# Gate and up of four SwiGLU layers: the high and low parts of the tokens beside each other, 512 moving columns at once

## The chip, the cores and the metric

The kernel runs on one core of one Trainium2 chip. The metric is the device time of one execution in microseconds (us), as the median of several runs. Smaller is better.

## The reference, cut to what matters

Two residual blocks run over 256 tokens of width 1024 in float32: in order a SwiGLU layer (here f1), an attention mixer (m1), a SwiGLU (f2), a second mixer (ab), a SwiGLU (f3), a third mixer (cd), a SwiGLU (f4) and a last norm. The change touches the four SwiGLU layers, each with a hidden width of 2816:

```python
D_MODEL = 1024
SEQ = 256
D_FF = 2816
def _swiglu(x, w_gate, w_up, w_down):
    return (jax.nn.silu(x @ w_gate) * (x @ w_up)) @ w_down
...
        f = _swiglu(_rmsnorm(x, ffn1_pre_g[l]), ffn1_w_gate[l], ffn1_w_up[l], ffn1_w_down[l])
        x = x + 0.5 * _rmsnorm(f, ffn1_post_g[l])
```

## The kernel before, in words

Every operand of a matmul is split in two float32r parts, a high one (`xh`, `wh`, `hh`) and a low one (`xl`, `wl`, `hl`), and each product is made of three matmuls: high by high, high by low, low by high (`mm3`, L506).

**Weights.** `Stream` loads weight tiles of 128x1024 (512 KB) in the order of a list (`ffn_specs`, L140) through SP's DMA queue. ACT casts each to `wh` (L91) and DVE, a few times POOL, subtracts to get `wl` (L96). There are 4 raw buffers and 6 of each part; `take(n)` (L111) hands out n tiles and emits the casts and subtractions that come into buffers which the tiles before have left.

**Tokens.** `enter` (L447) normalises, transposes through the PE (`to_t`, L353, tile `tp`) and writes `xh` (ACT, L364) and `xl` (DVE, L369), 128 partitions by 8 chunks of the width by 256 tokens, in two tiles (`new_xt`, L346).

**A SwiGLU layer** (`ffn`, L588) walks over 11 blocks of 256 hidden columns. Block 0 is computed inside `enter` by `first(h, mid)` (L604), once for each half h of the tokens: tokens stationary, weights moving with 256 columns, 48 matmuls into the bank `fh`, where `mid` puts the second half's transposes among the first half's matmuls. For blocks 1 to 10, `gemm_b` (L516) computes gate and then up with weights stationary and tokens moving: for each of two groups of 128 hidden columns 8 chunks by 3 products, so 48 matmuls of 256 columns, in one bank `gb`. Then ACT takes silu (L651), DVE multiplies by up (L652), ACT and DVE split the result into `hh` and `hl` (L622, L623), and `down` (L570) multiplies the block before with the down weights: 24 matmuls of 512 columns in the banks `f`. The last `down` takes the blocks 9 and 10 together.

In three of the four layers POOL copies `xh` and `xl` three times (L637, tile `xc`) to places chosen by byte offsets (`COPIES_AT`), and `act_x` picks one of the copies for each block. `XT_AT`, `COPY_PAD` and `HH_AT` are further offsets of tiles in a partition. `hooks` adds work of the later mixers behind some blocks of f1 and f3.

The order of each engine's work is that of the code. `ws.take` stands at the head of every `gemm_b` and `down`, so its casts and subtractions stand ahead of what the code emits later.

Of the kernel before, what the change touches and what calls it, by code (L numbers as in the profile page):

```python
# [8 lines left out]
F32 = mybir.dt.float32  # L9
# [5 lines left out]
P = 128  # L15
# [11 lines left out]


XT_AT = ((192, 240), (0, 256), (0, 256), (0, 0), (192, 240), (0, 256), (192, 192), (192, 240), (0, 256), (32, 32))
COPY_PAD = {0: 0, 1: 0, 3: 0}  # L30
HH_AT = (32, 32, 288, 32)

COPIES_AT = {0: ((192, 192), (64, 64), (320, 320)), 1: ((128, 128), (256, 256), (448, 192)),
             3: ((384, 384), (192, 320), (320, 64))}
# [105 lines left out]
def ffn_specs(wg, wu, wd):  # L140
    out = []
    d = w_d(wd)
    for j in range(11):
        out += w_b(wg, 256 * j) + w_b(wu, 256 * j)
        if 0 < j < 10:
            out += d[2 * j - 2:2 * j]
    return out + d[18:22]
# [43 lines left out]
class Kern:  # L191
    def __init__(self, ctx, tc, A, out, phases):
        self.ctx, self.tc, self.nc, self.A, self.out = ctx, tc, tc.nc, A, out
        self.phases = phases
        nc = self.nc
        pool = lambda n, b, **k: ctx.enter_context(tc.tile_pool(name=n, bufs=b, **k))
        self.const = pool("const", 1)
        self.w_raw = pool("wraw", NB_RAW)
        self.w_h = pool("wh", NB_HL)
        self.w_l = pool("wl", NB_HL)  # L200
        self.xt_p = pool("xt", 1)
        self.g_p = pool("gain", 2)
        self.tmp = pool("tmp", 2)
        self.sm = pool("sm", 4)
        self.mm_p = pool("mm", 8, space=bass.MemoryType.PSUM)
        self.specs = self.all_specs()
        self.ws = Stream(nc, (self.w_raw, self.w_h, self.w_l), self.specs)
        self.gains = {}
        self.bg = []
        self.fin = None  # L210
        self.after = 3

# [10 lines left out]
    def all_specs(self):  # L223
        A = self.A
        sp = []
        for ph in self.phases:
            if ph in ("f1", "f2"):
                k = ph[1]
                sp += ffn_specs(A[f"ffn{k}_w_gate"], A[f"ffn{k}_w_up"], A[f"ffn{k}_w_down"])
            elif ph in ("f3", "f4"):  # L230
                k = int(ph[1]) - 3
                sp += ffn_specs(A["ffn_w_gate_2"][k], A["ffn_w_up_2"][k], A["ffn_w_down_2"][k])
# [113 lines left out]
    def new_xt(self):  # L346

        self.nxt = getattr(self, "nxt", -1) + 1
        self.xh, self.xl = (
            self.xt_p.tile([P, 8 * S + 64], F32R, name=n, tag=n)[:, o // 4:o // 4 + 8 * S].rearrange("p (a t) -> p a t", a=8)  # L350
            for n, o in zip(("xh", "xl"), XT_AT[self.nxt]))

# [162 lines left out]

    def gemm_b(self, K=8, act=None):  # L516
# [71 lines left out]
    def ffn(self, gpre, gpost, coef, gnext, hooks=None, cut=False):  # L588
        nc = self.nc
        tt = nc.vector.tensor_tensor  # L590
        with self.tc.tile_pool(name="ffn", bufs=3) as fp:
            self.php = fp
            self.nff = getattr(self, "nff", -1) + 1
            fp.tile([P, HH_AT[self.nff] // 4], F32, name="gap", tag="gap", bufs=1)
            sets = {}
# [8 lines left out]
            def first(h, mid):  # L604
                if h == 0:
                    st["w"] = self.ws.take(4)
                p = self.ps(f"fh{h}")
                t = slice(h * P, (h + 1) * P)
                for i in range(2):
                    w = st["w"][2 * i:2 * i + 2]  # L610
                    prods = [((self.xh[:, k, t], self.xl[:, k, t]), (w[k // 4][0][:, k % 4, :], w[k // 4][1][:, k % 4, :]))
                             for k in range(8)]
                    self.mm3(p[:, i * S:(i + 1) * S], prods, True, True, True, mid if i else None)
                sg = fp.tile([P, S], F32, name="sgf", tag="sgf", bufs=2)
                nc.scalar.activation(out=sg, in_=p[:, 0:S], func=AF.Silu)
                tt(out=sg, in0=sg, in1=p[:, S:2 * S], op=ALU.mult)
                st[h] = sg

            def split(t, j):
                hh = fp.tile([P, 2, S], F32R, name="hh", tag="hh")  # L620
                hl = fp.tile([P, 2, S], F32R, name="hl", tag="hl")
# [3 lines left out]

            self.enter(gpre, first)
            self.gain(gnext)
            if gpost:
                self.gain(gpost)
            if self.nff in COPIES_AT:  # L630
                for n, at in enumerate(COPIES_AT[self.nff]):
                    sets[n] = []
                    for i, o in enumerate(at):
                        t = fp.tile([P, 8 * S + 128], F32R, name=f"xc{n}{i}", bufs=1)
                        o = (o + COPY_PAD[self.nff]) % 512 // 4
                        v = t[:, o:o + 8 * S].rearrange("p (a t) -> p a t", a=8)
                        nc.gpsimd.tensor_copy(out=v, in_=(self.xh, self.xl)[i])  # L637
                        sets[n].append(v)
            for j in range(1, 11):
                act_x = sets.get((j - 3) // 3)  # L640
                gt = self.gemm_b(act=act_x)
# [7 lines left out]
                up = self.gemm_b(act=act_x)  # L649
                sg = fp.tile([P, 2, S], F32, name="sg", tag="sg", bufs=2)  # L650
                nc.scalar.activation(out=sg, in_=gt, func=AF.Silu)  # L651
                tt(out=sg, in0=sg, in1=up, op=ALU.mult)  # L652
# [13 lines left out]
    def mixer1(self, gnext):  # L666
        nc, A = self.nc, self.A
        tt = nc.vector.tensor_tensor
        with ExitStack() as st:
# [4 lines left out]
            T([P, 8], "gap")  # L674
# [976 lines left out]
def _layout(inputs):  # L1651
# [4 lines left out]
    for n in ("ffn1_w_gate", "ffn1_w_up", "ffn1_w_down", "w_qkv", "w_out", "ffn2_w_gate", "ffn2_w_up", "ffn2_w_down", "x",  # L1656
              "ab_w_in_2", "ab_gate_a_w_2", "ab_gate_x_w_2", "ab_w_out_2", "cd_w_in_2", "cd_glu_w_2", "cd_w_out_2"):
        A[n] = A[n][0]
    rows = []
# [46 lines left out]
```

## Time and profile before

| | |
|---|---|
| runs | 1140.99 us median of 3 (1133.97 to 1141.59) |
| profiled execution, its own time | 1140.84 us |
| its span, first to last instruction | 1139.0 us |
| PE matmul busy | 1108.5 us (97%), 7435 instructions |
| PE weight load busy | 1008.6 us (89%) |
| DVE busy | 695.6 us (61%) |
| ACT busy | 547.5 us (48%) |
| POOL busy | 392.0 us (34%) |
| mean granted TensorE clock | 0.984 |

Busy time counts an instruction from its start to its end. Matmuls overlap in the pipeline, so the pace of the PE is read from the distance between starts, or from the chain of work that ended last, which counts each stretch once. A matmul named `gb<-xc,wh` writes the bank `gb` and reads `xc` and `wh`.

### The profile page before, as it was taken

The numbers are of one execution on the slowest core, as the hardware profiler recorded it, in microseconds if no ns is written. First come the engines' busy times: TensorE is split into PE (matmuls) and PEld (weight loads), VectorE is DVE, ScalarE is ACT, GpSimd is POOL, SyncE is SP. The second block draws the span as 40 slices with busy tenths as digits, with TensorE's granted clock in tenths as the row PEclk, the third lists the DMA queues.
The fourth block names the chain that finished last, engine by engine and source line by source line (L and its number), as shares of the span: only waits on it lengthen the run. The fifth ranks groups of instructions, "written<-read, shape, count | busy, mean of one in ns | idle before, by whom it ended". The sixth has DMA issues, their size and how long they took to land.

```text
span 1139.0 us, 18759 instructions
## 1 busy us (share of the span) xinstructions
PE 1108.5 (97%) x7435; PEld 1008.6 (89%) x7435; DVE 695.6 (61%) x828; ACT 547.5 (48%) x794; POOL 392.0 (34%) x590
## 2 busy tenths in 40 slices
PE   8999999989999999999989999999999999999997
PEld 7999999767889999997976999999989989999997
DVE  6765455789577554557573666556577557554554
ACT  4456445546555443445664544434353365443442
POOL 4206600655332000004151599999315126000000
PEclk9999999989999999999988999999999899999999
DMA  7865665642057556555621665575543335756551
GB/s 216 268 190 173 193 205 166 208 166 75 20 168 230 180 164 215 185 167 174 212 85 38 185 222 180 154 217 154 184 158 128 130 89 174 239 166 215 185 172 58
DMA packets 134361, 190.99 MB, mean 168 GB/s; under 512 B 6017, under 2 KB 109441, under 8 KB 134274
## 3 DMA queue, kind: packets, MB, share of 16 engines
q1 hardware_dynamic: 133536, 187.72, 52.5%
q0 software_dynamic: 736, 2.08, 0.7%
q8 instruction: 58, 0.95, 0.3%
q14 instruction: 29, 0.24, 0.1%
q10 hardware_dynamic: 2, 0.00, 0.0%
HBM read 188.73 MB, written 1.05 MB: 167 GB/s over the span
## 4 chain that ended last, share of the span: by engine, by line
PE 87%; DVE 5%; POOL 3%; issue 2%; ACT 1%; DMA 1%; SPq 0%; POOLq 0%; DVEq 0%; ACTq 0%
PE gb L514 45%; PE f L514 20%; PE wo L514 4%; PE fh L514 4%; PE ga L514 2%; PE gh L514 2%; PE o L842 1%; PE lg L514 1%; DVE x L397 1%; PE lt L1073 1%; DMA wraw<-in_ffn_w_up_dram 1%; PE y L1410 1%; PE pT L822 1%; PE M L1333 1%; PE sE L1379 1%
## 5 line engine op out<-in xcount | busy, mean ns | idle before, releaser
L96 DVE TENSOR_TENSOR wl<-wraw,wh 128x1024 fp32r<-128x1024 f32 x323 | 412.8, 1302 | 171.4 <-ACT wh L91 167.0
L91 ACT CAST wh<-wraw 128x1024 fp32r<-128x1024 f32 x341 | 349.3, 1049 | 213.8 <-PE gb L514 112.7
L514 PE MATMUL gb<-xc,wh 128*128 128x256 f32 x1536 | 274.3, 281 | 0.0
L514 PEld LDWEIGHTS gb<-xc,wh 128*128 128x128 f32 x1536 | 237.7, 188 | 1.9
L514 PE MATMUL gb<-xc,wl 128*128 128x256 f32 x768 | 216.3, 282 | 0.0
L514 PE MATMUL gb<-xh,wh 128*128 128x256 f32 x704 | 198.6, 282 | 0.0
L514 PE MATMUL gb<-xl,wh 128*128 128x256 f32 x704 | 197.4, 280 | 0.0
L514 PE MATMUL gb<-xh,wl 128*128 128x256 f32 x704 | 196.7, 279 | 0.0
L514 PEld LDWEIGHTS gb<-xc,wl 128*128 128x128 f32 x768 | 145.8, 190 | 0.0
L514 PE MATMUL f<-wh,hh 128*128 128x512 f32 x348 | 136.1, 391 | 0.0
L514 PE MATMUL f<-wh,hl 128*128 128x512 f32 x348 | 135.8, 390 | 0.0
L514 PE MATMUL f<-wl,hh 128*128 128x512 f32 x348 | 135.6, 390 | 0.0
L514 PEld LDWEIGHTS gb<-xh,wl 128*128 128x128 f32 x704 | 133.7, 190 | 0.0
L514 PEld LDWEIGHTS gb<-xl,wh 128*128 128x128 f32 x704 | 132.5, 188 | 0.6
L514 PEld LDWEIGHTS gb<-xh,wh 128*128 128x128 f32 x704 | 132.4, 188 | 0.7
L622 ACT CAST hh<-sg 128x512 fp32r<-128x512 f32 x40 | 24.8, 620 | 177.4 <-DVE sg L652 177.4
L652 DVE TENSOR_TENSOR sg<-sg,gb 128x512 f32<-128x512 f32 x40 | 27.4, 686 | 117.1 <-PE gb L514 116.4
L96 POOL TENSOR_TENSOR wl<-wraw,wh 128x1024 fp32r<-128x1024 f32 x21 | 57.3, 2735 | 87.1 <-ACT wh L91 84.4
L341 POOL TENSOR_TENSOR v<-ss 128x1 f32<-128x1 f32 x22 | 5.9, 269 | 234.3 <-ACT xs L333 167.9
L336 POOL TENSOR_SCALAR ss<-ss 128x1 f32<-128x1 f32 x6 | 1.7, 278 | 235.5 <-ACT xs L333 235.5
L514 PEld LDWEIGHTS f<-wh,hl 128*128 128x128 f32 x348 | 65.3, 188 | 14.3 <-DVE hl L623 0.4
L514 PEld LDWEIGHTS f<-wl,hh 128*128 128x128 f32 x348 | 65.4, 188 | 12.2
(414 smaller groups left out, 1715.2 us busy)
## 6 DMA issues: line engine op xcount, KB each, us to landing
wraw<-in_ffn_w_gate_dram SPq DMA_DIRECT2D x88, 512.0 KB, 4.0
wraw<-in_ffn_w_up_dram SPq DMA_DIRECT2D x88, 512.0 KB, 5.1
wraw<-in_ffn_w_down_dram SPq DMA_DIRECT2D x88, 512.0 KB, 4.2
wraw<-in_ab_w_in_dram SPq DMA_DIRECT2D x20, 512.0 KB, 4.7
wraw<-in_w_qkv_dram SPq DMA_DIRECT2D x18, 512.0 KB, 3.9
wraw<-in_cd_w_in_dram SPq DMA_DIRECT2D x16, 512.0 KB, 4.8
wraw<-in_w_out_dram SPq DMA_DIRECT2D x8, 512.0 KB, 4.2
wraw<-in_ab_w_out_dram SPq DMA_DIRECT2D x8, 512.0 KB, 3.6
```

The source lines that it names most:

```text
L91: self.nc.scalar.copy(out=h, in_=r)
L96: eng.tensor_tensor(out=l, in0=r, in1=h.bitcast(F32), op=ALU.subtract)
L397: nc.vector.scalar_tensor_tensor(out=xv[:, c], in0=t[:, c], scalar=r, in1=xv[:, c], op0=ALU.mult, op1=ALU.add)
L514: self.nc.tensor.matmul(out=out, lhsT=l, rhs=r, start=start and i == 0, stop=stop and i == n - 1)
L622: nc.scalar.copy(out=hh, in_=t)
L652: tt(out=sg, in0=sg, in1=up, op=ALU.mult)
L822: nc.tensor.transpose(p[:, k * S + h * P:k * S + (h + 1) * P], e[:, h, k * P:(k + 1) * P], self.ident)
L842: nc.tensor.matmul(out=o, lhsT=v, rhs=p, start=i % 2 == 0 and n == 0, stop=i % 2 == 1 and n == 5)
L1073: nc.tensor.matmul(out=p[:, 0:384], lhsT=tri[:, 0, :], rhs=s, start=True, stop=False, skip_group_check=True)
L1333: nc.tensor.matmul(out=pv[:, a, :], lhsT=l, rhs=F[:, a, 0:4, :].rearrange("p s q -> p (s q)"), start=r == 0, stop=r == 1)
L1379: nc.tensor.matmul(out=pv[:, r, a, :], lhsT=E[:, a, :], rhs=U[:, 4 * i + a, :], start=True, stop=True)
L1410: nc.tensor.matmul(out=o, lhsT=F[:, a, 1:5, :].rearrange("p s q -> p (s q)"), rhs=x[:, r, a, 0:64], start=False, stop=r == 1)
```

## The change

Tokens lie in one tile `xt`: for each of the 8 chunks 256 columns of `xh` and then 256 of `xl`, so that `x2[:, k, :]` has 512 columns. `gemm_b2` takes the place of `gemm_b` in the four SwiGLU layers: each high weight tile is loaded once and multiplies both parts (512 moving columns into a whole bank), and the low weight multiplies `xh` (256 columns) into the bank's second half. Each group of 128 hidden columns has a bank of its own, whose two halves `gather` adds: ACT copies the second half out of the bank, DVE adds the first. Block 0's gate and up weights lie beside each other in a new input `w_first`, so that `first` moves 512 columns as well. POOL's copies go, and the offsets of the tiles are new.

```diff
+WL_AT = 192
+XT_AT = ((0, 8384), (0, 8384), (8384, 176), (0, 8384), (8384, 176), (0, 8384))
+HH_AT = (352, 352, 96, 352)
...
-def ffn_specs(wg, wu, wd):
-    out = []
+def ffn_specs(w0, wg, wu, wd):
+    out = w_a(w0, 0)
     d = w_d(wd)
-    for j in range(11):
+    for j in range(1, 11):
...
+        gap = lambda n, b: pool(n, 1).tile([P, b // 4], F32, name=n)
+        gap("gap0", WL_AT)
         self.w_l = pool("wl", NB_HL)
+        gap("gap1", 512 - WL_AT)
...
     def new_xt(self):
+        t = self.xt_p.tile([P, 16 * S + WL_AT // 4], F32R, name="xt", tag="xt")
+        if self.pair_xt:
+            o = WL_AT // 4
+            self.x2 = t[:, o:o + 16 * S].rearrange("p (a x) -> p a x", a=8)
+            self.xh, self.xl = self.x2[:, :, 0:S], self.x2[:, :, S:2 * S]
+            return
...
+    def gemm_b2(self):
+        tiles = self.ws.take(2)
+        out = []
+        for j in range(2):
+            p = self.ps("gb")
+            c = slice(j * P, (j + 1) * P)
+            for k in range(8):
+                wh, wl = tiles[k // 4]
+                self.nc.tensor.matmul(out=p, lhsT=wh[:, k % 4, c], rhs=self.x2[:, k, :], start=k == 0, stop=False,
+                                      skip_group_check=True)
+                self.nc.tensor.matmul(out=p[:, S:2 * S], lhsT=wl[:, k % 4, c], rhs=self.xh[:, k, :], start=False,
+                                      stop=k == 7, skip_group_check=True)
+            self.pump(1)
+            out.append(p.rearrange("p (x t) -> p x t", x=2))
+        return out
...
             def first(h, mid):
-                for i in range(2):
-                    w = st["w"][2 * i:2 * i + 2]
-                    prods = [((self.xh[:, k, t], self.xl[:, k, t]), (w[k // 4][0][:, k % 4, :], w[k // 4][1][:, k % 4, :]))
-                             for k in range(8)]
-                    self.mm3(p[:, i * S:(i + 1) * S], prods, True, True, True, mid if i else None)
+                w = st["w"]
+                ops = [(self.xh[:, 2 * i + k, t], w[i][x][:, k, :]) for i in range(4) for x in range(2) for k in range(2)]
+                ops += [(self.xl[:, k, t], w[k // 2][0][:, k % 2, :]) for k in range(8)]
+                for n, (l, r) in enumerate(ops):
+                    if mid and n == 24 - 12 // self.after:
+                        mid()
+                    nc.tensor.matmul(out=p, lhsT=l, rhs=r, start=n == 0, stop=n == 23)
...
+            def gather(t, banks):
+                for c, p in enumerate(banks):
+                    nc.scalar.copy(out=t[:, c, :], in_=p[:, 1, :])
+                    tt(out=t[:, c, :], in0=p[:, 0, :], in1=t[:, c, :], op=ALU.add)
...
-                        nc.gpsimd.tensor_copy(out=v, in_=(self.xh, self.xl)[i])
...
             for j in range(1, 11):
-                act_x = sets.get((j - 3) // 3)
-                gt = self.gemm_b(act=act_x)
+                sg = fp.tile([P, 2, S], F32, name="sg", tag="sg", bufs=1)
+                su = fp.tile([P, 2, S], F32, name="su", tag="su", bufs=1)
+                gather(sg, self.gemm_b2())
+                nc.scalar.activation(out=sg, in_=sg, func=AF.Silu)
...
-                up = self.gemm_b(act=act_x)
-                sg = fp.tile([P, 2, S], F32, name="sg", tag="sg", bufs=2)
-                nc.scalar.activation(out=sg, in_=gt, func=AF.Silu)
-                tt(out=sg, in0=sg, in1=up, op=ALU.mult)
+                gather(su, self.gemm_b2())
+                tt(out=sg, in0=sg, in1=su, op=ALU.mult)
                 split(sg, j)
```

How the PE's order changes at the end of block 0 and the start of block 1 of f1, the kernel before (`fh1` is the bank of the second half of the tokens, the numbers tell tiles apart):

```order
L514 MATMUL fh1_264<-wl_179,xh_149 128x256 x4
L514 MATMUL fh1_264<-wh_163,xl_150 128x256 x4
L514 MATMUL fh1_264<-wh_178,xl_150 128x256 x4
L514 MATMUL gb_356<-xh_149,wh_252 128x256
L514 MATMUL gb_356<-xl_150,wh_252 128x256
L514 MATMUL gb_356<-xh_149,wl_253 128x256
```

The same place of the kernel after:

```order
L642 MATMUL fh1_247<-wl_186,xt_157 128x512 x2
L642 MATMUL fh1_247<-wh_141,xt_157 128x512 x2
L642 MATMUL fh1_247<-wh_149,xt_157 128x512 x2
L642 MATMUL fh1_247<-wh_170,xt_157 128x512 x2
L642 MATMUL fh1_247<-wh_185,xt_157 128x512 x2
L535 MATMUL gb_305<-xt_157,wh_235 128x512
L537 MATMUL gb_305<-xt_157,wl_236 128x256
```

In block 0 the eight matmuls with the low tokens now stand last, behind sixteen of 512 columns, and every matmul is twice as wide. In gate and up a pair of one 512 and one 256 column matmul takes the place of three of 256.

ACT's order in block 3 of f1, between the gate's matmuls and the split, before (`wh` are casts of weight tiles, `gb_719` is the gate's bank):

```order
L91 CAST wh_768<-wraw_675 128x1024
L91 CAST wh_774<-wraw_681 128x1024
L651 ACT_TABLE_LOAD
L651 ACTIVATE sg_829<-gb_719 128x512
L622 CAST hh_832<-sg_829 128x512
```

The same place after (`gb_627` and `gb_644` are the gate's two banks, `gb_678` and `gb_695` those of up):

```order
L659 COPY sg_613<-gb_627 128x256
L659 COPY sg_613<-gb_644 128x256
L671 ACT_TABLE_LOAD
L671 ACTIVATE sg_613<-sg_613 128x512
L89 CAST wh_666<-wraw_581 128x1024
L89 CAST wh_672<-wraw_587 128x1024
L659 COPY su_614<-gb_678 128x256
L659 COPY su_614<-gb_695 128x256
L653 CAST hh_717<-sg_613 128x512
```

Four copies out of PSUM are new, and the two casts that up's `take` emits now stand behind the gate's copies and its silu instead of ahead of the silu.

## Rows read from the trace of the kernel before

**Rows 1.** The page's chain that ended last: shares by engine and by line.
```profile
PE 87%; DVE 5%; POOL 3%; issue 2%; ACT 1%; DMA 1%; SPq 0%; POOLq 0%; DVEq 0%; ACTq 0%
PE gb L514 45%; PE f L514 20%; PE wo L514 4%; PE fh L514 4%; PE ga L514 2%; PE gh L514 2%; PE o L842 1%; PE lg L514 1%; DVE x L397 1%; PE lt L1073 1%; DMA wraw<-in_ffn_w_up_dram 1%; PE y L1410 1%; PE pT L822 1%; PE M L1333 1%; PE sE L1379 1%
```

**Rows 2.** The chain in order of time: start us, us, what (xN instructions).
```profile
93.79 11.31 PE gb L514 x96
105.10 5.44 PE f L514 x24
...
188.99 6.21 PE f L514 x28
...
334.89 0.87 PE tp L361 x8
...
376.42 11.52 PE gb L514 x96
...
735.45 5.49 PE f L514 x24
...
975.11 11.20 PE gb L514 x96
```

**Rows 3.** PE's order of time where down meets the next gate, in f2.
```profile
376.03 0.39 PE L514 MATMUL f<-wh,hl 128*128 128x512 f32 x1
376.26 0.40 PE L514 MATMUL gb<-xc,wh 128*128 128x256 f32 x2
```

**Rows 4.** Busy time of each engine in one block of f1.
```profile
core 0: us, PE busy (x) PEld busy (x) DVE busy (x) ACT busy (x) POOL busy (x), PEclk, DMA share, GB/s
60.30:77.04 16.74, 16.74 (x122) 15.81 (x122) 11.09 (x12) 8.95 (x10) 0.00 (x0) 1.00 0.63 193
```

**Rows 5.** Readers of gb, by tile: duration ns min/median/max, first and last start.
```profile
L651 ACT ACTIVATE sg<-gb x40: 583/589/597, 37.5 to 1116.4; 128x512 f32<-128x512 f32 x40
...
L985 ACT COPY xr<-gb x4: 373/378/381, 538.5 to 544.4; 128x256 f32<-128x256 f32 x4
```

**Rows 6.** Writers of sgf (block 0), by tile, columns as in rows 5.
```profile
L616 DVE TENSOR_TENSOR sgf<-sgf,fh x8: 407/417/423, 21.2 to 958.4; 128x256 f32<-128x256 f32 x8
```

**Rows 7.** ACT and DVE behind a gate and behind a block with hooks, f1.
```profile
82.66 1.05 ACT L91 CAST wh<-wraw 128x1024 fp32r<-128x1024 f32 x1 [0.37 <-PE gb L514]
83.75 1.22 DVE L96 TENSOR_TENSOR wl<-wraw,wh 128x1024 fp32r<-128x1024 f32 x1 [0.20 <-ACT wh L91]
...
95.44 4.75 DVE L96 TENSOR_TENSOR wl<-wraw,wh 128x1024 fp32r<-128x1024 f32 x4 [4.91 <-ACT wh L91]
```

**Rows 8.** The start of f2: PE, POOL and DVE in order of time.
```profile
326.89 2.39 POOL L96 TENSOR_TENSOR wl<-wraw,wh 128x1024 fp32r<-128x1024 f32 x1
327.05 1.30 PE L514 MATMUL fh<-wh,xh 128*128 128x256 f32 x8
330.42 1.27 DVE L369 TENSOR_TENSOR xl<-tp,xh 128x512 fp32r<-128x512 f32 x2
331.15 1.34 PE L514 MATMUL fh<-wh,xl 128*128 128x256 f32 x8 [1.85 <-DVE xl L369]
332.20 1.41 DVE L414 SCALAR_TENSOR_TENSOR xs<-x,r,g_ffn_pre_g 128x512 f32<-128x512 f32 x2 [0.50 <-POOL r L343]
336.08 1.15 PE L514 MATMUL fh<-wh,xh 128*128 128x256 f32 x8
```

**Rows 9.** The start of f1: PE and DVE.
```profile
13.52 1.91 PE L514 MATMUL fh<-wl,xh 128*128 128x256 f32 x8
14.76 2.35 DVE L96 TENSOR_TENSOR wl<-wraw,wh 128x1024 fp32r<-128x1024 f32 x2
17.03 1.40 DVE L414 SCALAR_TENSOR_TENSOR xs<-x,r,grow 128x512 f32<-128x512 f32 x2
```

**Rows 10.** The last multiplication and split of f1.
```profile
189.10 0.69 DVE L652 TENSOR_TENSOR sg<-sg,gb 128x512 f32<-128x512 f32 x1 [3.49 <-PE gb L514]
...
190.47 0.69 DVE L623 TENSOR_TENSOR hl<-sg,hh 128x512 fp32r<-128x512 f32 x1 [0.69 <-ACT hh L622]
```

More of the change, by code (lines that the diff above doesn't have):

```diff
@@ L25 @@
 MAGIC = 12582912.0
[L29 to L34, printed above, removed]
+WL_AT = 192
+XT_AT = ((0, 8384), (0, 8384), (8384, 176), (0, 8384), (8384, 176), (0, 8384))
+HH_AT = (352, 352, 96, 352)
 NB_RAW = 4
@@ L137, in w_d @@
     return [(v[:, i:i + 1, :], (1, 1024)) for i in range(v.shape[1])]
-def ffn_specs(wg, wu, wd):
-    out = []
+def ffn_specs(w0, wg, wu, wd):
+    out = w_a(w0, 0)
     d = w_d(wd)
-    for j in range(11):
+    for j in range(1, 11):
         out += w_b(wg, 256 * j) + w_b(wu, 256 * j)
-        if 0 < j < 10:
+        if j < 10:
             out += d[2 * j - 2:2 * j]
@@ L211, in __init__ @@
         self.after = 3
+        self.pair_xt = False
+        self.nxt = 0
     def pump(self, n):
@@ L228, in all_specs @@
                 k = ph[1]
-                sp += ffn_specs(A[f"ffn{k}_w_gate"], A[f"ffn{k}_w_up"], A[f"ffn{k}_w_down"])
+                sp += ffn_specs(A["w_first"][int(k) - 1], A[f"ffn{k}_w_gate"], A[f"ffn{k}_w_up"], A[f"ffn{k}_w_down"])
             elif ph in ("f3", "f4"):
                 k = int(ph[1]) - 3
-                sp += ffn_specs(A["ffn_w_gate_2"][k], A["ffn_w_up_2"][k], A["ffn_w_down_2"][k])
+                sp += ffn_specs(A["w_first"][2 + k], A["ffn_w_gate_2"][k], A["ffn_w_up_2"][k], A["ffn_w_down_2"][k])
             elif ph == "m1":
@@ L346, in new_xt @@
     def new_xt(self):
[L348 to L351, printed above, removed]
+        t = self.xt_p.tile([P, 16 * S + WL_AT // 4], F32R, name="xt", tag="xt")
[4 more added lines that the diff above has]
+            return
+        oh, ol = XT_AT[self.nxt]
+        self.nxt += 1
+        self.xh, self.xl = (t[:, o:o + 8 * S].rearrange("p (a t) -> p a t", a=8) for o in (oh // 4, ol // 4))
     def to_t(self, h, src, oh, ol, n=8):
@@ L592, in ffn @@
             self.php = fp
+            self.pair_xt = True
             self.nff = getattr(self, "nff", -1) + 1
-            fp.tile([P, HH_AT[self.nff] // 4], F32, name="gap", tag="gap", bufs=1)
-            sets = {}
+            fp.tile([P, HH_AT[self.nff] // 4], F32, name="gap2", tag="gap2", bufs=1)
             hts = {}
@@ L620, in split @@
                 hh = fp.tile([P, 2, S], F32R, name="hh", tag="hh")
+                if not hts:
+                    fp.tile([P, WL_AT // 4], F32, name="gap3", tag="gap3", bufs=1)
                 hl = fp.tile([P, 2, S], F32R, name="hl", tag="hl")
@@ L624, in split @@
                 hts[j] = (hh, hl)
+            def gather(t, banks):
+                for c, p in enumerate(banks):
+                    nc.scalar.copy(out=t[:, c, :], in_=p[:, 1, :])
+                    tt(out=t[:, c, :], in0=p[:, 0, :], in1=t[:, c, :], op=ALU.add)
             self.enter(gpre, first)
+            self.pair_xt = False
             self.gain(gnext)
@@ L629, in ffn @@
                 self.gain(gpost)
[L630 to L636, printed above, removed]
-                        nc.gpsimd.tensor_copy(out=v, in_=(self.xh, self.xl)[i])
-                        sets[n].append(v)
             for j in range(1, 11):
-                act_x = sets.get((j - 3) // 3)
-                gt = self.gemm_b(act=act_x)
+                sg = fp.tile([P, 2, S], F32, name="sg", tag="sg", bufs=1)
+                su = fp.tile([P, 2, S], F32, name="su", tag="su", bufs=1)
+                gather(sg, self.gemm_b2())
+                nc.scalar.activation(out=sg, in_=sg, func=AF.Silu)
                 if j == 1:
@@ L673, in mixer1 @@
             T = lambda sh, n, dt=F32: mp.tile(sh, dt, name=n)
-            T([P, 8], "gap")
             rope = T([P, 2, 4, 64], "rope")
@@ L1658, in _layout @@
         A[n] = A[n][0]
+    A["w_first"] = np.stack([np.concatenate([a[:, 0:256], b[:, 0:256]], 1) for a, b in (
+        (A["ffn1_w_gate"], A["ffn1_w_up"]), (A["ffn2_w_gate"], A["ffn2_w_up"]),
+        (A["ffn_w_gate_2"][0], A["ffn_w_up_2"][0]), (A["ffn_w_gate_2"][1], A["ffn_w_up_2"][1]))])
     rows = []
```

## The prediction

> **What bounds the kernel now.** I read the chain of waits first, by engine and line. The PE holds 87% of it, and 45% of the span is one line with one tile, `gb` (gate and up, and the mixers' calls of the same function), 20% is `f`, the down product [rows 1]. The same chain in order of time shows how steady this is: gate and up of one block are 96 matmuls in 11.31 us, down is 24 in 5.44 us, with nothing between them [rows 2]. So within a layer only the PE's pace counts, and a wait that ends on another engine costs nothing as long as the PE does not meet it. I then read the pace: 11.31/96 = 117.8 ns for 256 moving columns, 5.44/24 = 226.7 ns for 512. At the full clock of 2.4 GHz the columns alone are 106.7 and 213.3 ns, so the rows leave 11.1 and 13.4 ns per instruction beside them. That is what fewer, wider matmuls can save. The pace of 256 columns is not everywhere the same: 11.52/96 = 120.0 ns in f2 and 11.20/96 = 116.7 ns in f4 [rows 2], in stretches that read different copies of the tokens, at other byte offsets. Last I read ACT and DVE in one block, which get the new work: 8.95 and 11.09 us busy of 16.74 [rows 4], in the block where hooks add most.
>
> **Gate and up.** Per group of 128 hidden columns and chunk, three matmuls of 256 columns become one of 512 and one of 256: the same columns, one instruction less. Per gemm 48 become 16 + 16, per pair of gemms 96 become 32 + 32. Before, the 40 pairs take 454.2 us on the chain: 23 pairs at 11.31, 12 at 11.52, and the five others (at starts and in f4) at 11.16 in the mean; the first and last kind are in rows 2. After, by the paces of the rows: 32 x 226.7 + 32 x 117.8 = 11.02 us, times 40 = 441.0. Gain 13.2 us. No row shows a 512 into a whole bank followed by a 256 into half of the same bank; the nearest is the seam between down and the next gate, where the start after a 512 comes 0.23 us later, so a 512 keeps its pace before a 256 [rows 3]. Bounds: the tiles get new offsets, so I take for the 256 anything from 113 ns (the 116.7 of f4 less the distance to 120.0) to 120.0 and for the 512 226.7 to 228.8 (the slowest down, 5.49/24): gain 19 to 7.7 us (64 instructions x 40 pairs each). I take 226.7 and 117.8, the paces of the most rows.
>
> The Trainium skill, in "TensorE: Matmul & The Clock Gate", section "Back-to-back issue gap", gives an isolated warm matmul N/2.4 + 2.5 ns. By it this edit would save 16 x 2.5 ns per gemm, 80 x 0.04 = 3.2 us in all. The trace does not agree: 117.8 ns where the page has 109.2, 226.7 where it has 215.8.
>
> **Block 0.** `first` goes from 48 matmuls of 256 to 24 of 512 per half: 48 x 117.8 = 5.65 us to 24 x 226.7 = 5.44, times 8 halves: 1.7 us. The order changes too. In f2 the PE waits 1.85 us for `xl`, 16 matmuls in, because DVE is late; the first half's `xl` is written by 331.1 (330.42 and half of 1.27) [rows 8]. After, sixteen 512s stand ahead of `xl`: 327.05 + 16 x 0.227 = 330.68, a wait of 0.45. What comes late next is the second half's `xs`, ready at 332.20 + 1.41 = 333.61, which the transposes need; behind them (8 in 0.87 us [rows 2]) two 512s stand, so the half ends at 333.61 + 0.87 + 0.45 = 334.95 against 336.08: 1.1 us. In exchange the fourth low weight tile is needed after 14 matmuls, 330.2, where POOL has it at 326.89 + 2.39 = 329.28 [rows 8]: no wait. In f3 and f4 no such wait stands now, and I count none. At the start of f1 it is a draw at zero: low weight tiles 3 and 4 leave DVE at about 15.9 and 17.1, and the new order needs each right behind its high tile, so the PE will stand in pieces there; but the second half's `xs` comes at 17.03 + 1.40 = 18.43 either way and holds the half's end. The PE still runs at half pace there (8 matmuls in 1.91 us where 8 of f2 take 1.34 or less [rows 8, 9], so the level of 1.2 GHz). Bounds: 0.5 us gained, 2.5 us lost if the gaps let the clock rise eleven 512s later (0.227 us more for each).
>
> **The gather.** Per block 4 copies of 128x256 out of PSUM on ACT, 0.378 us each [rows 5], and 4 additions on DVE, 0.417 each [rows 6]: 1.5 and 1.7 us more per block, 60 and 67 us in all. ACT comes to 10.5 of 16.5 us at most and DVE to 12.8 [rows 4]; the PE's 11.0 + 5.4 us per block hide them. What could be late is the order: the two casts of up's `take` now queue on ACT behind the gate's last copy, DVE's addition and silu. At one gate's end the second cast began at 82.66, as its buffer came free [rows 7]; it would begin about 0.38 + 0.42 + 0.59 + 1.05 us plus seams, 2.6 us, later, and its subtraction end at 87.6 instead of 84.97. The PE wants that tile two takes on, in the gate at 93.79: 6 us in hand. The tightest place is behind the hooks of f1: the first of four subtractions starts at 95.44, so the first two end at 96.6 and 97.8 [rows 7], for an up that starts at 93.79 + 5.65 = 99.44 and wants the second tile 1.4 us later. A split that ends 1 us later leaves 1.8. So I cost this at nothing; if that cover were gone, each block would pay what is missing.
>
> At a layer's end it is close. Multiplication, cast and subtraction run 189.10 to 191.16 [rows 10], from a down that starts at 188.99 [rows 2] and wants `hh` of block 10 after 12 matmuls (2.72 us) and `hl` after 14 (3.17). The gather's last copy and addition put 0.38 + 0.42 + seams ahead: `hl` at 188.99 + 2.17 + 0.9 = 3.07 us in. I take 0.1 us of wait for each of 4 layers, 0.4 us; bounds 0 and 0.4 each.
>
> **Others.** POOL's eighteen copies go; nothing waits for them but the matmuls that read them, and no PE wait there stands in the chain. DVE's subtractions beside them get quicker, which is hidden. The mixers' gemms keep their shapes at new offsets: zero, bounds 2 us either way. The bytes loaded are the same.
>
> **Sum.** 13.2 + 1.7 + 1.1 - 0.4 = 15.6 us. The profiled execution took 1140.84 us (span 1139.0), as good as the median of 1140.99, so 1125.2; I say 1125.
>
> **Rivals.** (1) What lies above the column time goes with the columns or the weight bytes streamed beside them, not with the instruction. For: the pace moves with the offsets of what is read. Against: `f` at 226.7 is less than 2 x 117.8 = 235.6. Then the 512 over tokens costs 235.6, gate and up and block 0 gain nothing, and f2's 1.1 less 0.4 leaves 1140. The page's formula, with only 2.5 ns per instruction, lands in the same place by another way. Chance 0.2. (2) The new offsets fit better than the old: 113 ns for every 256. For: 116.7 is there now. Gain 19 + 2.8 - 0.4, 1119.5. Chance 0.15. (3) Weights come late. ACT's longer chain behind each gate holds the casts back, these the subtractions, these the raw buffers and the next loads, until the PE meets an unfinished `wl` in every block. For: the chain does grow by 2.6 us at one take of three. Against: 6 us in hand. It turns the sign from 15.6/40 = 0.39 us per block; with 1 us in each of 40 blocks it gives 1165. Chance 0.06. The forecast has the rest, 0.59.
>
> **How the numbers follow.** A measurement of this kernel tells about 1%, 11.4 us, from no change, so faster means below 1129.6. Forecast (its own range 1120 to 1131) with nine tenths, rival 2 whole: 0.68. Same: rival 1 and the slow edge of the forecast, 0.26. Slower: rival 3, 0.06. The range goes from rival 2 less a spread of runs (one run of three before was 7 us under the median), 1114, to the slow bounds together (7.7 + 1.7 + 1.1 - 1.6 - 2.5 - 2 = 4.4, 1136.4), 1137.
>
> **What would show it.** In the chain of the changed kernel gate and up of a block should be 64 matmuls in 11.0 us; 11.3 speaks for rival 1, under 10.9 for rival 2. Down should stay at 24 in 5.44. In f2 the wait for `xl` should be near 0.45 us. Waits of the PE for `wl` (DVE, ACT's casts) in blocks 2 to 10 would be rival 3. I am wrong if a 512 behind a 256 in the same bank is slower than 226.7 by more than 12 ns (15.6 us over 1280 pairs).

## The result, and the profile after

The changed kernel takes 1125.2 us (median of 4 runs, 1124.27 to 1126.38), beside 1141.14 us of the kernel before (4 runs, 1133.97 to 1141.59): ratio 0.9875, 95% interval 0.9835 to 0.9915. Predicted were 1125 us, range 1114 to 1137. Below, the kernel before is called before and the changed one after. The profiled execution took 1124.95 us, its span 1123.2 (before 1140.84 and 1139.0).

Part of this difference is not the change's: the profiled execution of before has 10.2 us at half the clock in mixer cd, which that of after has not (nine of this case's fourteen profiles have it, those of e7 at 1124.28 and e10 at 1122.05 us among them), and 70 later runs of before have a median of 1136.1 us (34 of them at a mean granted clock of 0.989, 1132.7 to 1136.2 us; 24 at 0.984, as the profiled one, 1139.3 to 1142.7 us). Against that median the gain is 10.9 us.

The page of after: busy time, and the chain by engine and by line.

```profile
PE 1094.8 (97%) x5963; PEld 926.4 (82%) x5963; DVE 743.5 (66%) x988; ACT 598.9 (53%) x954; POOL 357.3 (32%) x572
...
PE 84%; DVE 6%; POOL 3%; issue 2%; ACT 2%; DMA 1%; SPq 0%; POOLq 0%; DVEq 0%; ACTq 0%
PE gb L535 26%; PE f L523 21%; PE gb L537 13%; PE wo L523 4%; PE gb L523 4%; PE fh L642 3%; PE gh L523 2%; PE ga L523 1%; PE o L869 1%; PE lg L523 1%; PE lt L1100 1%; DVE x L406 1%; DMA wraw<-in_w_first_dram 1%; PE pT L849 1%; PE tp L370 1%
```

The chain is still the PE's. The 45% of `gb` in [rows 1] are now 26% of 512 columns (L535), 13% of 256 (L537) and 4% of the mixers (L523). Down (`f`) has grown from 20% to 21%. The chain of after in order of time: start us, us, what.

```profile
54.31 5.57 PE f L523 x24
70.77 5.57 PE f L523 x24
...
185.99 6.34 PE f L523 x28
...
306.14 11.18 PE wo L523 x48
...
614.37 16.99 PE wo L523 x72
```

From one down to the next are 16.46 us; less 5.57, gate and up take 10.89 us, against 11.31 and 11.52 in [rows 2]. But down itself takes 5.57 us, against 5.44 and 5.49 there, and the last 28 take 6.34 against 6.21. The PE in order of time inside a gate shows where the gain sits:

```profile
94.92 0.28 PE L537 MATMUL gb<-xt,wl 128*128 128x256 f32 x1
95.03 0.39 PE L535 MATMUL gb<-xt,wh 128*128 128x512 f32 x1
95.25 0.28 PE L537 MATMUL gb<-xt,wl 128*128 128x256 f32 x1
95.37 0.39 PE L535 MATMUL gb<-xt,wh 128*128 128x512 f32 x1
```

The next start comes 0.22 to 0.23 us after a 512 and 0.11 to 0.12 after a 256: 0.34 us a pair (10.89 / 32), where the prediction had 0.2267 + 0.1178 = 0.3445.

The same block by engines (us, PE, PEld, DVE, ACT, POOL busy, PEclk, DMA share, GB/s), and the PE's waits for weights in the whole span (us in all, times, longest):

```profile
54.31:70.77 16.46, 16.46 (x90) 14.14 (x89) 11.47 (x25) 11.10 (x15) 0.00 (x0) 1.00 0.55 186
```

```profile
PE wo L523 <- POOL wl L94: 1.0, 1, 1.0
...
PE fh L642 <- POOL wl L94: 0.8, 1, 0.8
...
PE fh L642 <- DVE wl L94: 0.3, 1, 0.3
```

No row names gate, up or down: rival 3 did not come. The start of f2 in order of time, which answers to [rows 8]:

```profile
328.16 1.28 DVE L378 TENSOR_TENSOR xt<-tp,xt 128x512 fp32r<-128x512 f32 x2
328.89 1.23 PEld L642 LDWEIGHTS fh<-wh,xt 128*128 128x128 f32 x6 [0.75 <-DVE xt L378]
328.89 1.66 PE L642 MATMUL fh<-wh,xt 128*128 128x512 f32 x6 [0.33 <-DVE xt L378]
329.94 1.41 DVE L423 SCALAR_TENSOR_TENSOR xs<-x,r,g_ffn_pre_g 128x512 f32<-128x512 f32 x2 [0.50 <-POOL r L346]
330.75 0.42 PEld L370 LDWEIGHTS tp<-ident,xs 128*128 128x128 f32 x4 [0.62 <-DVE xs L423]
330.75 1.32 PE L370 MATMUL tp<-ident,xs 128*128 128x128 f32 x8 [0.20 <-DVE xs L423]
```

The wait for the low tokens is 0.33 us (before 1.85, forecast 0.45), and `xs` is the next to be late, by 0.20.

Last the clock. Busy time of each engine in a stretch of cd, the kernel before (the number behind POOL's is the granted clock):

```profile
883.50:893.90 10.40, 10.40 (x43) 9.66 (x43) 4.60 (x10) 0.00 (x0) 0.39 (x2) 0.51 0.32 102
```

And after, over the part of cd behind the same place:

```profile
884.00:925.00 41.00, 39.42 (x232) 33.50 (x231) 24.70 (x37) 23.86 (x41) 7.76 (x5) 1.00 0.34 112
```

### The profile page after: what moved, and what is told of

It is laid out like the page before. It is cut to its first block, busy times and chain, and to the rows that moved or that the text cites. A ratio compares the mean times of both kernels' runs of the same rounds, so it can differ in the third digit from the quotient of the medians.

```text
span 1123.2 us, 16090 instructions
## 1 busy us (share of the span) xinstructions
PE 1094.8 (97%) x5963; PEld 926.4 (82%) x5963; DVE 743.5 (66%) x988; ACT 598.9 (53%) x954; POOL 357.3 (32%) x572
## 4 chain that ended last, share of the span: by engine, by line
PE 84%; DVE 6%; POOL 3%; issue 2%; ACT 2%; DMA 1%; SPq 0%; POOLq 0%; DVEq 0%; ACTq 0%
PE gb L535 26%; PE f L523 21%; PE gb L537 13%; PE wo L523 4%; PE gb L523 4%; PE fh L642 3%; PE gh L523 2%; PE ga L523 1%; PE o L869 1%; PE lg L523 1%; PE lt L1100 1%; DVE x L406 1%; DMA wraw<-in_w_first_dram 1%; PE pT L849 1%; PE tp L370 1%
## 5 line engine op out<-in xcount | busy, mean ns | idle before, releaser
L535 PE MATMUL gb<-xt,wh 128*128 128x512 f32 x1280 | 439.1, 390 | 0.0
L537 PE MATMUL gb<-xt,wl 128*128 128x256 f32 x1280 | 353.9, 277 | 0.0
L535 PEld LDWEIGHTS gb<-xt,wh 128*128 128x128 f32 x1280 | 240.3, 188 | 50.6
L537 PEld LDWEIGHTS gb<-xt,wl 128*128 128x128 f32 x1280 | 240.5, 188 | 1.7
L523 PE MATMUL f<-wh,hh 128*128 128x512 f32 x348 | 138.2, 397 | 0.0
L523 PE MATMUL f<-wh,hl 128*128 128x512 f32 x348 | 137.1, 394 | 0.0
L523 PE MATMUL f<-wl,hh 128*128 128x512 f32 x348 | 136.9, 393 | 0.0
L659 ACT COPY sg<-gb 128x256 f32<-128x256 f32 x80 | 29.8, 373 | 140.5 <-PE gb L537 137.2
L660 DVE TENSOR_TENSOR sg<-gb,sg 128x256 f32<-128x256 f32 x80 | 33.4, 423 | 94.4 <-ACT sg L659 94.2
L523 PEld LDWEIGHTS f<-wh,hl 128*128 128x128 f32 x348 | 65.3, 188 | 16.8 <-DVE hl L654 0.9
L523 PEld LDWEIGHTS f<-wh,hh 128*128 128x128 f32 x348 | 65.4, 188 | 14.6
L523 PEld LDWEIGHTS f<-wl,hh 128*128 128x128 f32 x348 | 65.4, 188 | 13.3
L523 PE MATMUL gb<-xt,wh 128*128 128x256 f32 x384 | 69.1, 282 | 0.0
L659 ACT COPY su<-gb 128x256 f32<-128x256 f32 x80 | 29.2, 368 | 64.7 <-PE gb L537 64.7
L523 PEld LDWEIGHTS gb<-xt,wh 128*128 128x128 f32 x384 | 59.4, 188 | 0.4
L523 PE MATMUL gb<-xt,wl 128*128 128x256 f32 x192 | 54.3, 283 | 0.0
L523 PE MATMUL wo<-wh,xt 128*128 128x512 f32 x160 | 52.6, 400 | 0.0
```

The costliest lines, as they stand in the source:

```text
L523: self.nc.tensor.matmul(out=out, lhsT=l, rhs=r, start=start and i == 0, stop=stop and i == n - 1)
L535: self.nc.tensor.matmul(out=p, lhsT=wh[:, k % 4, c], rhs=self.x2[:, k, :], start=k == 0, stop=False, skip_group_check=True)
L537: self.nc.tensor.matmul(out=p[:, S:2 * S], lhsT=wl[:, k % 4, c], rhs=self.xh[:, k, :], start=False, stop=k == 7, skip_group_check=True)
L659: nc.scalar.copy(out=t[:, c, :], in_=p[:, 1, :])
L660: tt(out=t[:, c, :], in0=p[:, 0, :], in1=t[:, c, :], op=ALU.add)
```

## The experiments

Each run is after with one edit; e1 to e12 are their labels. Time of gate and up of a block is read as above: from the end of one down to the start of the next, in f1's blocks without hooks. Sums over the four layers are taken from the starts of the matmuls.

### Fewer instructions, or other offsets?

The first question: does the gain come from the instruction that is saved, or from the tiles' new places? The offsets of the tiles in a partition (mod 512 bytes, from the built programs) were 160 for `wh`, `wl`, `hh` and `hl` before; after, `wh` and `hh` are at 160 and `wl`, `hl` and the tokens `xt` at 352, 192 bytes on. First run: after, with each 512 made in two 256.

```diff
-                self.nc.tensor.matmul(out=p, lhsT=wh[:, k % 4, c], rhs=self.x2[:, k, :], start=k == 0, stop=False, ...
+                for x in range(2):
+                    t = slice(x * S, (x + 1) * S)
+                    self.nc.tensor.matmul(out=p[:, t], lhsT=wh[:, k % 4, c], rhs=self.x2[:, k, t],
+                                          start=k == 0 and x == 0, stop=False, skip_group_check=True)
```

> The changed kernel, but each 512-column matmul of gate and up is cut in two of 256 with the same high weight loaded twice, at the changed kernel's own offsets. Theory A (the gain is one instruction less per chunk, each costs some 11 ns beside its columns): three 256 per chunk go back to 113 to 118 ns each, 340 to 352 ns against 340 for the pair now; a block's gate and up is 11.0 to 11.3 us instead of 10.88, and the time 1130 to 1142. Theory B (the gain is the new offsets, any count of instructions would have it): 10.9 us per block and 1125, no change.

Measured: 1140.49 us (10 runs, 1137.31 to 1141.3), ratio to before 1.0023 (1.0002 to 1.0044). Its chain:

```profile
54.81 5.57 PE f L523 x24
71.68 5.57 PE f L523 x24
```

71.68 - 54.81 - 5.57 = 11.30 us: 117.7 ns for each of 96, as before, at the new offsets. Over the four layers gate and up sum to 452.3 us, against 454.2 in before and 437.0 in after. So the new offsets alone bring gate and up next to nothing, and what the change gains there hangs on the wider matmul. Down stays at 5.57 without the wider matmul, so its loss does not come from that; how much of it the offsets make, the next two runs show.

Second and third run: the instructions of after at other offsets. In e2 `wl`, `hl` and `xt` lie at the offset of `wh`; in e3 the tokens alone are 192 bytes on.

```diff
-WL_AT = 192
+WL_AT = 0
+X_AT = 0
...
-HH_AT = (352, 352, 96, 352)
+HH_AT = (32, 32, 288, 32)
```

> The changed kernel's instructions with the offsets of the kernel before: low weights, tokens and the split hidden tiles at the same place modulo 512 bytes as the high weights. Theory A (instructions count; the shift of 192 bytes between high and low weights is a trade: it makes the 256 of gate and up quick, 113 ns, and down slow, 232 ns): down returns to 5.44 us per block, gate and up go to 16 x 2 x 2 x (227 + 118 to 120) = 11.04 to 11.09 us, and the two nearly cancel: 1122 to 1128. Theory B (the gain is the offsets): gate and up return to 11.3 us, 1135 or more.

> As the run with the old offsets, but the tokens' tile of the four layers stands 192 bytes off all weights. Theory A with a quick 256 whenever its tokens are 192 bytes from the next weight: down 5.44 us and gate and up 10.9 us per block, so faster than both kernels, 1116 to 1119. Theory A with the pace set by both neighbours: 256 at 118 and 512 at 227 to 233, gate and up 11.0 to 11.2 us, 1120 to 1128. Theory B: gate and up near 11.3 us, 1135.

Measured: e2 1134.61 us (1131.93 to 1139.6), ratio 0.9981 (0.9956 to 1.0006); e3 1136.83 us, 1.0008 (0.9990 to 1.0026). The chain of e2:

```profile
54.03 5.50 PE f L526 x24
70.82 5.50 PE f L526 x24
...
307.97 10.92 PE wo L526 x48
...
620.40 16.59 PE wo L526 x72
```

Gate and up take 70.82 - 54.03 - 5.50 = 11.29 us in e2 and 11.30 in e3: a pair of 512 and 256 takes 353 ns, what three 256 take (353). The saved instruction alone brings next to nothing either, at these offsets (e2 sums to 452.0 us): theory B of both expectations. Down takes 5.50 in e2 and 5.47 in e3, so the old offsets give back 0.07 to 0.10 of the 0.13 us that it lost, and not all of it. And the mixers' `wo`, 10.92 and 16.59 us, are what the kernel before shows, against 11.18 and 16.99 in after: the mixers pay for the shift too.

Fifth run: only the weights are shifted, `xt` and `hl` lie with `wh` and `hh`.

```diff
-            o = WL_AT // 4
+            o = 0
...
-                if not hts:
+                if not hts and HL_AT:
```

> As the changed kernel, with the low weights still 192 bytes (mod 512) behind the high ones, but the SwiGLU layers' tokens at the offset of the high weights and hl at that of hh. Theory A (it is the shift between the two weights that a 512 behind a 256 needs): gate and up of a block stay at 10.9 us, and down, whose two stationary parts now lie alike, comes back towards 5.44 from 5.57; time about 1120 to 1124 us. Theory B (the tokens must lie at the low weights' offset too): gate and up at 11.3, time near 1136 to 1140. Theory C on down alone (it pays for the shift between the weights that it moves, whatever hl does): down stays at 5.57.

Measured: 1136.38 us, ratio 0.9997 (0.9976 to 1.0019). Gate and up 11.23, down 5.51. On gate and up theory B comes nearest. Down is better than in after, and not at 5.44: theory A has the direction on down, not the size.

Seventh run: 64 bytes in the place of 192 everywhere (`WL_AT = 64`).

> As the changed kernel, with 64 bytes in the place of 192 for the shift of wl, of the tokens and of hl. Theory A (any shift that keeps the two streams apart does): gate and up 10.9 us a block, time near 1125. Theory B (the distance itself counts): gate and up between 10.9 and 11.3, and down other than 5.57; without any gain 1138.

Measured: 1123.84 us (1122.08 to 1124.8), ratio 0.9874 (0.9826 to 0.9921). Gate and up 10.90, down 5.53: theory A. So far it looked as if the shift of tokens and low weights together were the cause.

### The same matmuls at the same addresses, at two paces

Sixth run: it was meant for down alone, and it took that reading away. Down makes its products in three groups for each half of the tokens; every matmul of gate and up keeps its operands' addresses.

```diff
+            if not last:
+                for x, y in ((0, 0), (1, 0), (0, 1)):
+                    for i in range(n):
+                        for b, c in b2:
+                            k = chunk + i
+                            self.nc.tensor.matmul(out=accs[h][b], lhsT=act(k)[x][:, t], rhs=tiles[i][y][:, 0, c], ...
+                continue
```

> As the changed kernel, but down (all but a layer's last) makes its 24 products in three groups for each half of the tokens: four of wh by hh, four of wh by hl, four of wl by hh, instead of the three in turn. Theory A (the offset of what is moved or loaded changing from one matmul to the next is what down pays): inside a group 227 ns, at its ends 232 to 236, so down at 5.46 to 5.49 instead of 5.57, 40 downs, some 3 to 4 us less, 1121. Theory B (down pays for something else, the denser copies and casts beside it): 5.57 stays, 1125.

Measured: 1137.18 us (1135.2 to 1139.43), ratio 0.9989 (0.9965 to 1.0013): neither. Its chain:

```profile
54.00 5.54 PE f L612 x24
...
70.75 5.54 PE f L612 x24
```

Down gains 0.03 us, and gate and up go to 70.75 - 54.00 - 5.54 = 11.21 us: 350 ns a pair in place of 340. The offsets are the same, so they are not the whole cause. After itself shows both paces. Its chain through block 1 of f1 (gate, four transposes `ft`, up, down):

```profile
26.36 0.23 PE gb L535
26.71 0.23 PE gb L535
...
31.61 0.23 PE gb L535
31.96 0.44 PE ft L676 x4
32.40 0.23 PE gb L535
...
37.51 0.23 PE gb L535
37.85 5.57 PE f L523 x24
```

Gate: 31.61 - 26.36 = 5.25 us for 15 pairs, 350 ns each. Up: 37.51 - 32.40 = 5.11 us, 341 ns each, with the same shapes and offsets. Up to here the PE's instructions in e6 are the same from the program's first on, addresses included; there this up takes the longer pace as well. Busy time in that up, after:

```profile
32.40:37.85 5.45, 5.45 (x34) 4.82 (x33) 3.56 (x5) 3.39 (x6) 0.00 (x0) 1.00 0.98 330
```

And e6:

```profile
31.65:37.25 5.60, 5.60 (x34) 4.92 (x33) 3.44 (x5) 3.37 (x5) 0.00 (x0) 1.00 1.00 321
```

The granted clock is 1.00 in both, DVE and ACT do nearly the same work, and the PE waits for nothing: 5.45 and 5.60 us. Start by start, from the second pair on, the shorter up reads 341, 340, 340, 340 ns and stays there; the longer alternates between 348 and 352 ns to its end. A rhythm is here the pattern of distances between starts that a stream of matmuls settles in and then repeats. At these addresses there are at least three: 340 ns a pair, 348 and 352 (or 349 and 351) by turns, and 350 and 357 by turns, which the first gate of f3 and of f4 keeps in after (5.65 us). From the second block on every block of after settles in the first, and every block of e6 in the second (theory R below).

What picks it? Three runs on down's order. e9 turns the last two matmuls of each down:

```diff
+                if not last and h == b == i == 1:
+                    for n, (l, r) in enumerate(((ah, wh), (al, wh), (ah, wl))):
+                        self.nc.tensor.matmul(out=accs[h][b], lhsT=l[:, t], rhs=r[:, 0, c], start=False, ...
+                    continue
```

> As the changed kernel, with the last two of the 24 matmuls of each down (but a layer's last down) in turned order: wh by hl and then wl by hh. Every matmul of gate and up is the same, at the same addresses. Theory R (gate and up settle in one of several rhythms, and how they are entered picks it): the pairs of a 512 and a 256 take 350 ns instead of 340, gate and up of a block 11.2 us, time near 1136. Theory O (the byte offsets alone set the pace, and the grouped down slowed gate and up in some other way): 10.88 us stays, time 1125.

Measured: 1124.93 us (1123.2 to 1125.66), ratio 0.9878 (0.9834 to 0.9922), gate and up 10.89: the number of theory O. Theory R in the form that the last two pick the rhythm is wrong. e11 is the grouped down with its last two groups exchanged (`((0, 0), (0, 1), (1, 0))` in the diff of e6):

> As the grouped down, but with the groups in the order wh by hh, wl by hh, wh by hl, so that the last matmul ahead of gate is wh by hl as in the changed kernel. Theory R: if the last matmul alone picks the rhythm, gate and up are back at 10.88 us and the time is near 1124 with down at 5.54; if what stands further ahead counts too, 11.2 may stay. Theory O with the grouped down as the culprit: 11.2 stays for certain, time 1136.

Measured: 1136.54 us (1133.78 to 1139.06), ratio 0.9984 (0.9959 to 1.0009), gate and up 11.20. Both theories allow that. e12 groups only the first half of the tokens, so that the twelve matmuls ahead of gate are again those of after (`if not last and h == 0:` in the diff of e6):

> As the changed kernel, with down grouped for the first half of the tokens only: its second half, the twelve matmuls straight ahead of gate, is word for word that of the changed kernel. Theory R (gate and up settle in one of two rhythms at the same addresses, and what the PE runs just ahead picks it): 10.88 us a block, time 1122 to 1126. Theory G (the grouped order slows gate and up wherever it stands in down, by something other than the entry): 11.2 us a block, 1136.

Measured: 1120.66 us (1116.88 to 1125.33), ratio 0.9875 (0.9823 to 0.9927). The chain:

```profile
53.57 2.77 PE f L612 x12
56.34 2.78 PE f L523 x12
70.01 2.77 PE f L612 x12
```

70.01 - 53.57 - 5.55 = 10.89 us, the shorter rhythm: theory R, and grouping as such is not what slows gate and up. The order of the last two matmuls ahead of gate does not pick the rhythm (e9), and the last twelve in the order of after are enough to keep the shorter one (e12). Which of the twelve decide, and by what inside the PE, stays open; it wasn't tried.

An obvious rival is that a grouped down frees its weight tiles at other moments, so that casts and subtractions beside gate start at others. The traces speak against it: in block 3 of f1, until gate's first group is done, ACT and DVE start each of their instructions at the same distance from gate's first matmul in after, e6 and e12, to 0.04 us. ACT's casts start 1.73 and 0.79 us ahead of it and 0.16 behind in after, 1.70, 0.76 and 0.18 in e6; yet the pairs take 340 ns in after and e12 and 350 in e6.

Nor is the PE's order the whole cause. In block 1 of f1 the PE's instructions are the same in after, e4, e6, e9, e11 and e12 up to the end of up, and up settles at 340 ns in after and at 350 in the other five. What picked it there no run shows.

### The cover of the gather, and the order in block 0

e4 doubles the suspected cost: each copy out of PSUM and each addition of the gather is followed by a second instruction of the same size.

```diff
                     nc.scalar.copy(out=t[:, c, :], in_=p[:, 1, :])
+                    nc.scalar.copy(out=t[:, c, :], in_=p[:, 1, :])
                     tt(out=t[:, c, :], in0=p[:, 0, :], in1=t[:, c, :], op=ALU.add)
+                    tt(out=t[:, c, :], in0=t[:, c, :], in1=t[:, c, :], op=ALU.max)
```

> The changed kernel with ACT's copy out of the bank done twice and a second DVE instruction behind each addition (same result): 4 more on each engine per block. Theory A (ACT and DVE are covered by the PE): gate, up and down keep their pace, at most 0.3 us more at each layer's end, 1125 to 1127. Rival (weights come late once ACT's chain grows): waits of the PE for weight tiles in the blocks, 0.4 us or more per block, 1141 or more.

Measured: 1139.05 us (1135.04 to 1140.34), ratio 1.0009 (0.9983 to 1.0034). In the blocks of f1, f2 and f4 nothing moves: 10.89 and 5.57 us. The waits of the PE have one new row:

```profile
PE f L523 <- ACT hh L653: 5.6, 4, 4.0
```

The PE now meets the split at the four layer ends: the last two downs take 12.70 us in f1 (11.69 in after), about 1.0 us more in each of three layers, and 17.02 against 11.23 in f3, where mixer work stands ahead of it on ACT and DVE and where the clock fell to half for 3.4 us behind the 4.0 us of wait. The blocks of f3 with hooks grow by 0.2 to 0.4 us. Theory A took 0.3 us for a layer's end, which was too little; the waits for weight tiles of the rival did not come. The ends and f3's blocks make 10.2 us; the rest of the 13.9 us between the medians is not taken apart, but this execution has the stretch at half clock in cd as well. So the gather of after is hidden, in the blocks with much in hand, at the layer ends with next to nothing.

e8 gives block 0 its old order of products at the new width.

```diff
-                ops = [(self.xh[:, 2 * i + k, t], w[i][x][:, k, :]) for i in range(4) for x in range(2) for k in range(2)]
-                ops += [(self.xl[:, k, t], w[k // 2][0][:, k % 2, :]) for k in range(8)]
+                ops = []
+                for g in ((0, 1), (2, 3)):
+                    ops += [(self.xh[:, 2 * i + k, t], w[i][x][:, k, :]) for x in range(2) for i in g for k in range(2)]
+                    ops += [(self.xl[:, 2 * i + k, t], w[i][0][:, k, :]) for i in g for k in range(2)]
```

> As the changed kernel, but block 0 multiplies the low tokens in the old places: for each half of the chunks 16 matmuls... behind eight 512s instead of sixteen. Theory A (the order is what took f2's wait for xl away): in f2 the PE waits 1.7 to 1.9 us for xl again, and from the first fh to the first gb there are 16.5 to 17 us instead of 15.75, about 1 us more in all, within what the times tell apart (1125 to 1126). Theory B (the second half's xs sets the end in any case): the wait comes back, the stretch does not get longer.

Measured: 1124.97 us (1122.88 to 1126.77), ratio 0.9887 (0.9846 to 0.9927). The PE at the start of f2:

```profile
329.74 2.13 PE L644 MATMUL fh<-wh,xt 128*128 128x512 f32 x8 [2.19 <-DVE xt L378]
```

The wait is back, 2.19 us. The 15.75 us in the expectation are counted from the first `xs` (322.33) to the first gate (338.08); here they run from 323.19 to 340.18, 16.99. Theory A: the order is worth 1.2 us in f2 (and 0.8 in f1, where first `fh` to first `gb` takes 17.00 us and 16.24 in after), too little to be seen in the times.

e8 also shows what an entry does: behind block 0's old order the first gate of each of the four layers settles at 340 ns a pair. Its chain in f1:

```profile
27.00 0.23 PE gb L535
...
32.45 0.44 PE ft L678 x4
```

32.45 - 27.00 = 5.45 us, against 5.60 to 5.65 in after. The up behind it then takes the rhythm of 350 and 357, so gate and up sum to 436.6 us in all (437.0 in after).

### A version with a quicker down

e10 is after with `hl` at the offset of `hh` (the gap between them goes, `if not hts and HL_AT:` with `HL_AT = 0`).

> As the changed kernel, with hl at the offset of hh (the 192 bytes between them taken out). Down as in the run with only the weights shifted, 5.51 us instead of 5.57. Theory R: it also changes how gate is entered, so gate and up are at either 10.88 (then 1122 us in all) or 11.2 (1134). Theory O: 10.88 for certain, 1122.

Measured: 1122.74 us (1122.05 to 1125.12), ratio to before 0.9865 (0.9827 to 0.9902). Down is at 5.53, gate and up stay in the shorter rhythm at 10.87. Over the four layers that is 436.5 us of gate and up (437.0 in after) and 243.3 of down (245.5): 2.7 us less than after. The medians lie 2.5 us apart, but the intervals of the two ratios overlap (0.9835 to 0.9915 for after), so the chains carry this and not the times. Both theories allow 10.87. e12's median is lower still, but its profiled execution ran at a mean clock of 0.994 (after 0.988), and by its chain (437.2 and 244.5) it is worth 0.8 us over after.

## Why the prediction was right, point by point

The total was right to 0.2 us, and the terms were not. That they cancel to 0.2 us is luck, and so is the rhythm that gate and up settled in. Summed from the traces over the four layers (down with the matmuls that hooks put between f3's blocks, 10.6 us in both kernels):

| term | predicted gain, us | measured, us |
|---|---|---|
| gate and up, 40 pairs | 13.2 | 17.2 (454.2 to 437.0) |
| down | 0 | -4.7 (240.8 to 245.5) |
| block 0 | 2.8 | 2.0 |
| layer ends | -0.4 | none seen |
| mixers, at their own pace | 0, bounds 2 | -2.6 |
| half clock in cd, in this execution of before | not in the sum | 4.0 |
| sum | 15.6 | 15.9 |

**Gate and up.** "I take 226.7 and 117.8, the paces of the most rows": in the rhythm of after a 512 keeps its pace ahead of a 256, 227 ns, as was forecast, but the 256 took 113 ns, the lower bound, which is rival 2's pace. This half of the pair is mis-sized. By the sign that the prediction gave, 10.89 us is just under 10.9, so this is rival 2's case in this one term. But there was no pace of 117.8 to be had: behind a 512 the pair settles at 340 or 350 ns, and 344.5 lies between. And the mechanism, that each saved instruction gives its 11 ns back, holds in the shortest rhythm alone. In the longer one of e6 a 512 takes some 232 ns and a 256 118, gate and up sum to 448.5 us, a gain of 5.7, and the kernel is no faster than before; e2, with as many instructions, gains 2.2. (The prediction counts 23 pairs at 11.31 us and 12 at 11.52 where the chain has 24 and 11; its sum holds to 0.2 us.)

**Down.** "Down should stay at 24 in 5.44" is the step that failed. It took 5.57, 0.13 us more in each. The offsets were bounded for gate and up and for the mixers, and not for down, whose moving weights and low stationary part were shifted as well. e2, with all offsets alike, has 5.50; start by start, its down opens at 224 to 241 ns and settles at 227, while that of after opens at 226 to 236 and settles at 236, 233, 231. So about half of the 0.13 us goes with the offsets; the other half comes in e2's opening, at offsets that are those of before, and why it opens slowly was not tried.

**Block 0.** f2 came out as worked out: 1.5 us from its own order and width (forecast 1.1 + 0.4), the wait 0.33 (0.45), `xs` late next, and e8 gave 1.2 of it back. f3 and f4 gained 0.26 and 0.33 (0.4 each). f1 lost 0.1, the draw that was forecast; its share of the width's gain went into waits.

**Gather.** Hidden in the blocks, as forecast: ACT 11.10 and DVE 11.47 us busy in 16.46 (forecast at most 10.5, and 12.8). At the layer ends the low part did come late, but only the weight load met it. The group on the page of after, with the idle time ahead of it:

```profile
L523 PEld LDWEIGHTS f<-wh,hl 128*128 128x128 f32 x348 | 65.3, 188 | 16.8 <-DVE hl L654 0.9
```

0.9 us of waits of the load in four layers (0.4 in before), and none of the PE. e4 shows how near that edge is.

**Mixers.** They lost 0.4 (m1), 1.6 (ab) and 0.6 us (cd). That is outside the bounds of 2: `wo` alone lost 0.26 and 0.40 us, and e2 has both back. In cd after is 3.4 us quicker than before, but only because before has the stretch at half clock. What the stretch costs can be read from the runs that have the mixers of after: from f3's last matmul to f4's first `fh` it is 106.5 to 106.6 us in the five profiles without the stretch (after, e1, e8, e9, e12) and 110.5 to 110.6 in five with it (e4, e5, e6, e10, e11), so 4.0 us; 3.4 less 4.0 is -0.6.

**The clock.** The base of the sum was one execution with the stretch in cd, and that put 4.0 us into the measured difference that no step had foreseen. It stands in the granted clock of that stretch, which the prediction did not read. Without it the terms give 11.9 us; the median of the 70 runs of before gives 1136.1 - 1125.2 = 10.9.

**The rivals.** Rival 1's outcome, no gain, came in e2, e3, e5, e6 and e11 (1134.6 to 1137.2 us, where the 70 runs of before have 1136.1), by a mechanism it did not name: a longer rhythm at the same instruction count. Its pace, 235.6 + 117.8 = 353.4 ns a pair, is near the 353 of e2 and e3, but down's 512s settle at 227 there, so the columns alone do not make it. Its chance of 0.2 was low, since in e6 and e11 the case that came hung on how gate is entered. The way by 2.5 ns per instruction, said to land in the same place, gives 3.2 + 0.5 + 1.1 - 0.4 = 4.4 us by the prediction's own terms, 1136.4. Rival 3 did not come in any block.

## What to carry to other kernels

Where the PE's pace bounds, read it matmul by matmul and in several places before carrying it over: a stream of matmuls settles in a rhythm, a small change ahead of it can move it to another, 3% apart here, and a whole edit can vanish in that. When tiles move, every stream that reads them has to be bounded, not only the one that the edit is for. And before a profiled execution serves as the base of a sum, look where its clock fell: a stretch that other runs do not have is no part of the change. A total that comes out right proves no term of the sum.

## What the runs showed of the hardware that was not expected

- The same 32 matmuls at the same addresses and at a granted clock of 1.00 take 5.45 us in one kernel and 5.60 in another whose PE instructions are the same up to there. The rhythms are steady: 340 ns a pair in one, 348 and 352 by turns in the other, over all 32 pairs of a block. What the PE runs just ahead can pick between them (e6, e12); yet in block 1 of f1, behind the same instructions, both came.
- Which rhythms were seen differs with the byte offsets: with tokens and low weights 192 or 64 bytes on, 340 or 350 ns (at 192 also 350 and 357 by turns); with all alike, 350, 350 and 360 by turns; with the tokens alone shifted, 353 and 354; with the weights alone, 346 to 356. No 340 settled in the last three, behind block 0, behind the transposes or behind down.
- 512 moving columns behind each other settle at 227 ns where all offsets are alike (before, e2), at 227 to 230 with the low weights 192 bytes on and `hl` not (e5, e10), and at 231 to 236 with the low weights and `hl` 192 bytes on.
- In e4, behind a wait of 4.0 us at the end of f3, the granted clock fell to half for 3.4 us, where the changed kernel, without the wait, kept the full one.
- 10.2 us at half clock in cd made the mixer 4.0 us longer (106.5 and 110.5 us), less than half of the stretch.
